# Sixty-four experts' weights in 2 MB transfers with 16 KB runs, VectorE's block transpose for the hidden layer, and a ring of ten matrices

## The chip, the cores and the metric

The kernel runs on one core of a Trainium2 chip. The metric is the device time of one execution in microseconds; the time before is the median of three runs. One execution was also recorded by the hardware profiler, and all rows below are from that record. In it PE is TensorE's matmul stream, PEld its weight loads, DVE is VectorE, ACT ScalarE, POOL GpSimd, and SP is SyncE, whose queue issues nearly all DMA transfers.

## The reference

One layer of a streaming encoder on 256 tokens of 1024 features, float32: a gated merge of two recurrent branches, a cross-attention over 256 memory tokens, and a mixture of 64 experts, of which each token takes two. The change lies in the last part:

```
def expert_block(args):
    xb, e = args
    hid = jax.nn.silu(xb @ w_gate[e]) * (xb @ w_up[e])      # [1024, 512] each
    return hid @ w_down[e]                                   # [512, 1024]
```

The router takes the best group of eight experts and in it the best two; their rows come back weighted, and a last RMS norm follows. Each of an expert's three matrices has 2 MB (2,097,152 bytes), so all experts have 402.65 MB, and every expert is computed whether tokens chose it or not.

## The kernel before

**Stages.** Projections, branches, merge, attention and router take the first part of the span. Their weights go through two buffers named `raw` (L162), are split in two by ACT, DVE and POOL (`whl`, L169 and L170), and are used by PE (L178 to L180). Then the experts run one after the other, 0 to 63, each on 32 slots for tokens. An `overflow` loop (L1190, L1191) ahead of them takes experts with more tokens than slots; here it makes no pass that counts.

**One expert** (`expert`, L1150). `gate_up` (L1094) multiplies the tokens with gate, then with up, eight tiles of the features each, with four ranges of 128 columns on four quarters of the array. `hidden` takes silu(gate) * up: ACT's tanh (L1102), two DVE instructions (L1103, L1104), a PE transpose into PSUM (L1106) and an ACT copy back (L1107). `down` (L1115) multiplies with the third matrix, `to_rows` (L1120) copies the result to rows. After every fourth expert, `combine` (L1126 to L1131) adds four experts' rows to the tokens' sums and `prepare` gathers the next four experts' tokens (`gather`, L1077 to L1088). The last expert's `down` goes by four ranges of columns (`LAST`), so that its end can start before its last bytes land (`last`, L1267 to L1285).

**The ring.** The weights come through a ring of 21 places of 1 MB, 8 KB of each partition: nine (`ra`) where the early stages' buffers were, twelve (`rb`) where the middle stages' buffers were. `order` lists the twelve in the order in which what was there before is done with: places 0 to 2 were single buffers, 3 and 4 `raw`, 5 to 8 `whl`, 9 to 11 those of the attention. `load_next` (L1061, L1063, L1067) fetches half a matrix: for gate and up, 8 KB of each partition that lie together in memory; for down, two pieces of 4 KB (hidden row j * 128 + p on partition p). 21 halves are issued ahead of the experts, six more after each expert, all from SP, in the order of use. A place's next transfer waits until PE has read what is in it, and a transfer also waits until the one eight places earlier in the queue has landed.

**What sets the order.** The instructions' order on each engine is chosen by a planner at build time, by its own costs; each engine then runs its queue in order and waits on semaphores. SP's queue therefore holds the ring's first transfers between the `raw` loads of the attention's weights, where the planner put them.

The lines that matter:

```
if i < 2:
    nc.sync.dma_start(t, src.rearrange("(p c) f -> p (c f)", p=128)[:, h * 2048:h * 2048 + 2048])
elif e < NE - 1:
    nc.sync.dma_start(t.rearrange("p (j n) -> p j n", j=2),
                      src[h * 256:h * 256 + 256].rearrange("(j p) n -> p j n", p=128))
```

Of the kernel before, what the change touches and what calls it, by code (L numbers as in the profile page):

```python
# [8 lines left out]
FT = mybir.dt.float32  # L9
# [13 lines left out]
# columns of the constants' arrays: for the whole, and for what comes before the attention  # L23
# [12 lines left out]
# columns of the small parameters' array  # L36
# [5 lines left out]
def hybrid_kernel(ctx: ExitStack, tc: tile.TileContext, A, out, dbg=None, until=99):  # L42
# [45 lines left out]
    def bcast(ap, n):  # L88
        """ap[p, w] as [p, n, w], each alike."""
        return ap.rearrange("p (o w) -> p o w", o=1).to_broadcast([ap.shape[0], n, ap.shape[1]])  # L90

    def spread(ap, n):
        """ap[p, w] as [p, w, n], each element n times."""
        return ap.rearrange("p (w o) -> p w o", o=1).to_broadcast([ap.shape[0], ap.shape[1], n])
# [32 lines left out]
    def rsqrt_columns(ys, xs, ts, y, x):  # L127
        """-8192 / sqrt(x) of x's columns xs, two instructions a step: the scale is squared away last."""
# [7 lines left out]
    def softplus(dst, x, t0, t1, t2):  # L136
        """max(x, 0) + log(1 + e), e = exp(-|x|), log(1 + e) = 2 atanh(e / (2 + e)) by its series."""
# [19 lines left out]
    def load_w(src, k=8, m=256, hi=(SC, SC), lo=(V, G), loads=1):  # L157
        """A unit of weights, [128, k, m], loaded and split: piece i // (k / 2) has its k-tile i."""
# [15 lines left out]
    def dense(p, w, m, u, k=8):  # L174
        """p[128 outputs of tile m, 256 tokens]; u(half, k-tile) is [128, 256]."""
# [6 lines left out]
    def dense_two(w, u):  # L182
        """Both tiles of a unit, a bank each, with what comes last of u used last."""
# [10 lines left out]
    def act(pair):  # L194
        """Halves in two tiles [128, 2048] as dense() takes them."""
        h = [t.rearrange("p (c t) -> p c t", c=8) for t in pair]
        return lambda s, i: h[s][:, i]
# [10 lines left out]
    def square_sums(xt, name):  # L208
        """[128 features of a tile, 256 tokens], summed over the tiles."""
# [7 lines left out]
    def rs_rows(x):  # L217
        """1 / RMS of each token, a row on every partition."""
# [52 lines left out]
    X = small("xg", [3, 2, 8])            # g cumulated in the chunk; g to its end; 2 beta  # L271
# [17 lines left out]
    EGL = small("egl", [2, 2, 8])         # exp of a chunk's whole decay: tile, half, head  # L289
    SC.activation(EGL.rearrange("p t c h -> p (t c h)"), pg[:, 32:64], AF.Exp)  # L290
    # A unit is a pair of heads and a chunk, a head on each half of the partitions:
    # [(head of the pair, token), quantity, (tile, pair, chunk of the tile)]
# [8 lines left out]
    TM = small("tm", [6, 16])             # g, g to the end, 2 beta, exp of the first two, -exp(g) / 4  # L301
# [52 lines left out]
    gg = [five("gg0"), five("gg1")]       # 2 gelu(rg)  # L354
# [15 lines left out]
    for h in range(2):  # L370
# [8 lines left out]
        # log a = ch (tr + 1), ch = -4 softplus(-lambda); -expm1(log a) = (1 + exp(log a)) tanh(-log a / 2)  # L379
# [5 lines left out]
        V.scalar_tensor_tensor(tr, a, 1.0, tr, op0=OP.add, op1=OP.mult)             # 1 - a  # L385
        V.tensor_scalar(a, tr, -1.0, 1.0, op0=OP.mult, op1=OP.add)
        V.scalar_tensor_tensor(tr, tr, -2.0, tr, op0=OP.add, op1=OP.mult)           # a^2 - 1
        # halved twice: for the gate's and for the gelu's halves
# [44 lines left out]
    gb = single("gb", 0).rearrange("p (c t) -> p c t", c=8)                         # tanh(gB / 2)  # L433
# [15 lines left out]
    # [side, pair of heads, chunk, head of the pair, 64 tokens]  # L449
# [43 lines left out]
    # a quarter, as k is doubled  # L493
    V.tensor_scalar(NK[:, 0], NK[:, 0], 0.25, EPS, op0=OP.mult, op1=OP.add)
    rsqrt(NK[:, 2], NK[:, 0], NK[:, 3])
    V.tensor_mul(NK[:, 3], NK[:, 2], NK[:, 2])                       # 1 / (sum k^2 + eps)
    V.scalar_tensor_tensor(NK[:, 5], TM[:, 2], 0.5, NK[:, 3], op0=OP.mult, op1=OP.mult)
    V.tensor_scalar_mul(NK[:, 6], NK[:, 5], 0.25)
    V.scalar_tensor_tensor(NK[:, 4], NK[:, 0], 0.5, NK[:, 2], op0=OP.mult, op1=OP.mult)   # its root, for v, which is doubled

# [27 lines left out]
    # a tile's diagonal blocks of 16 in columns (column of the block, its place in its 32, unit)  # L528
# [40 lines left out]
    # what the tensor engine does while it waits for the inverses  # L569
# [10 lines left out]
    flat8 = lambda t: t.rearrange("p n i -> p (n i)")  # L580

    def products(a, b):
        """a^T b of every unit, a's heads as diagonal blocks: a bank for eight units."""
# [8 lines left out]
    for lev in (16, 32):  # L592
# [5 lines left out]
        for g in range(2):  # L598
            if lev == 16:
                V.tensor_copy(US[:, GR[g]], p[g])  # L600
                # the blocks inverted so far lie within 32 x 32
# [27 lines left out]
    # o stands 4 sqrt(128 (sum q^2 + eps)) too large: its norm's eps is scaled alike  # L629
# [25 lines left out]
    for c in range(4):  # L655
# [47 lines left out]
        # the head's RMS norm  # L703
# [12 lines left out]
    def y_of_b():  # L716
        """Branch B's y, from o transposed."""
# [24 lines left out]
    for c0, n in ((0, 2), (2, 2), (4, 2), (6, 1), (7, 1)):  # L742
# [7 lines left out]
        with tc.high_priority():  # L750
            t = t2k("mrg")[:, :n * 256].rearrange("p (m t) -> p m t", m=n)
            V.scalar_tensor_tensor(t, gb[:, q], 1.0, pv, op0=OP.add, op1=OP.mult)
            V.tensor_add(t, t, ya[:, q])                             # doubled
# [43 lines left out]
    def scores(hq):  # L797
        """Two heads' scores and their softmax over the memory."""
# [19 lines left out]
    def turned(h):  # L818
        """A head's probabilities, transposed."""
# [15 lines left out]
    for un_ in range(4):  # L835
# [9 lines left out]
        if un_ == 0:  # L845
# [5 lines left out]
            V.tensor_scalar_mul(rs2[:, 1], rs2[:, 1], 1.0 / 16)      # with the scores' scale  # L851
# [196 lines left out]
    def load_next():  # L1048
        """Half of a matrix of an expert: four tiles of the features, two of the hidden ones."""
        n = len(ring)  # L1050
        if n >= 6 * NE:
            return
# [338 lines left out]
```

## Time and profile before

| what | value |
|---|---|
| time, median of 3 runs | 1516.94 us (1515.17 to 1519.67) |
| profiled execution: span from first to last instruction | 1514.2 us |
| profiled execution: own time | given as its span alone; the median lies 2.7 us above it |
| PE busy | 1188.8 us, 79% of the span |
| DVE, ACT, POOL busy | 519.3, 367.8 and 197.6 us |
| DMA queue of SP | 472.57 MB in 84048 packets, 78.6% of 16 engines' span |
| mean granted TensorE clock | 0.851 of full speed |

The page cuts the span into 40 slices of 37.9 us each; a digit is the busy share in tenths. A packet is what one DMA engine moves in one piece. The chain of waits starts at the last instruction and goes back, at each step, to what released it. In lists of instructions, "x32" is the number merged into the row, and what stands in brackets is the idle time before it and what ended it.

### The profile page before, as it was taken

What the parts mean: (1) busy time and instruction counts of PE and PEld (TensorE: products, weight loads), DVE (VectorE), ACT (ScalarE), POOL (GpSimd) and SP (SyncE); (2) the same over time, 40 slices, a digit from 0 to 9 for tenths busy, and PEclk for the clock granted to TensorE, in tenths of its full rate; (3) what the DMA queues carried; (4) which work ended last, traced back from release to release, by engine and by line L of the source; (5) the groups of instructions that cost most, each with busy time, mean ns of one, the idle gap of its engine ahead of it and who ended that gap; (6) DMA issues with size and microseconds to landing.
All of it is one profiled execution on the core that took longest, in us unless ns stands there. A gap on an engine that the chain in (4) does not pass through costs nothing.

```text
span 1514.2 us, 33706 instructions
## 1 busy us (share of the span) xinstructions
PE 1188.8 (79%) x15005; PEld 926.6 (61%) x15005; DVE 519.3 (34%) x1153; ACT 367.8 (24%) x810; POOL 197.6 (13%) x107
## 2 busy tenths in 40 slices
PE   6899889889998979877677686776777766768675
PEld 6898889789798966655344453444545434445343
DVE  7867788674666431211011110111101101111022
ACT  5366655425444421110000000100000000000002
POOL 2343333531136210000000000000000000000000
PEclk9899999979999989998787877777868778777787
DMA  7353344421157869999999999999999999999995
GB/s 255 124 176 127 124 145 145 157 84 56 56 196 277 342 224 372 415 415 416 415 415 416 417 415 415 415 416 415 416 415 416 416 417 413 417 411 414 415 409 208
DMA packets 85492, 477.44 MB, mean 315 GB/s; under 512 B 7520, under 2 KB 10208, under 8 KB 45152
## 3 DMA queue, kind: packets, MB, share of 16 engines
q1 hardware_dynamic: 84048, 472.57, 78.6%
q8 instruction: 119, 1.95, 0.5%
q10 hardware_dynamic: 1296, 2.68, 0.5%
q14 instruction: 29, 0.24, 0.0%
HBM read 474.17 MB, written 1.05 MB: 314 GB/s over the span
## 4 chain that ended last, share of the span: by engine, by line
DMA 51%; PE 10%; ACT 1%; issue 1%; DVE 0%; DVEq 0%; SPq 0%; ACTq 0%
DMA rb<-weu 12%; DMA rb<-weg 9%; DMA rb<-wed 9%; DMA ra<-weg 8%; DMA ra<-weu 7%; DMA ra<-wed 5%; PE gd L1094 4%; PE gd L1085 2%; PE gd L1115 2%; PE mm L1131 1%; PE mm L1162 0%; PE sm L1077 0%; PE sm L1126 0%; ACT hid L1102 0%; PE gd L1106 0%
## 5 line engine op out<-in xcount | busy, mean ns | idle before, releaser
L1094 PE MATMUL gd<-rb,xy 128*32 128x128 f32 x4608 | 181.6, 314 | 89.2 <-DMA rb<-weu 53.2
L1094 PEld LDWEIGHTS gd<-rb,xy 128*32 128x32 f32 x4608 | 144.4, 125 | 131.9 <-DMA rb<-weu 69.7
L170 POOL TENSOR_TENSOR whl<-raw,whl 128x1024 fp32r<-128x1024 f32 (+1 forms) x66 | 159.6, 2419 | 341.9 <-ACT whl L169 341.8
L1094 PE MATMUL gd<-ra,xy 128*32 128x128 f32 x3456 | 139.0, 317 | 67.2 <-DMA ra<-weu 40.3
L1094 PEld LDWEIGHTS gd<-ra,xy 128*32 128x32 f32 x3456 | 109.9, 127 | 100.1 <-DMA ra<-weu 51.9
L178 PE MATMUL mm<-u1h,whl 128*128 128x256 f32 x544 | 162.6, 299 | 9.8 <-DVE cvt L313 9.8
L1103 DVE SCALAR_TENSOR_TENSOR hid<-hid,gd 128x128 f32<-128x128 f32 x64 | 18.4, 287 | 426.1 <-ACT hid L1102 426.1
L180 PE MATMUL mm<-u1h,whl 128*128 128x256 f32 x544 | 160.7, 295 | 2.6 <-DVE whl L170 2.5
L179 PE MATMUL mm<-u1l,whl 128*128 128x256 f32 x544 | 159.9, 294 | 0.0
L169 ACT CAST whl<-raw 128x1024 fp32r<-128x1024 f32 (+1 forms) x132 | 131.3, 1008 | 110.6 <-PE mm L180 84.4
L1120 DVE COPY xy<-gd 32x256 f32<-32x256 f32 x126 | 52.7, 418 | 233.2 <-PE gd L1115 211.8
L1102 ACT ACTIVATE hid<-gd 128x128 f32<-128x128 f32 x64 | 17.8, 278 | 460.0 <-PE gd L1094 460.0
L1120 ACT COPY xy<-gd 32x256 f32<-32x256 f32 x126 | 45.9, 364 | 303.6 <-DVE xy L1120 303.6
L1115 PE MATMUL gd<-rb,hid 128*32 128x256 f32 x1152 | 104.5, 511 | 16.4 <-ACT hid L1107 9.6
L178 PEld LDWEIGHTS mm<-u1h,whl 128*128 128x128 f32 x544 | 109.4, 201 | 12.3 <-issue 6.3
L180 PEld LDWEIGHTS mm<-u1h,whl 128*128 128x128 f32 x544 | 109.1, 201 | 5.0 <-DVE whl L170 2.9
L179 PEld LDWEIGHTS mm<-u1l,whl 128*128 128x128 f32 x544 | 109.2, 201 | 0.8 <-issue 0.2
L976 POOL TENSOR_TENSOR gpw<-goh,ew 128x512 f32<-128x512 f32 x8 | 8.4, 1048 | 745.7 <-PE sm L1126 702.5
L170 DVE TENSOR_TENSOR whl<-raw,whl 128x1024 fp32r<-128x1024 f32 (+1 forms) x66 | 85.0, 1289 | 58.9 <-ACT whl L169 58.6
L1115 PE MATMUL gd<-ra,hid 128*32 128x256 f32 x864 | 74.4, 491 | 11.2 <-ACT hid L1107 7.6
L1085 PEld LDWEIGHTS gd<-goh,hm 128*128 128x128 f32 x512 | 67.2, 203 | 23.5 <-issue 22.5
L1088 DVE SCALAR_TENSOR_TENSOR xy<-gd,vecs,rr 128x128 f32<-128x128 f32 x128 | 39.0, 346 | 123.1 <-PE gd L1085 123.0
(421 smaller groups left out, 1826.8 us busy)
## 6 DMA issues: line engine op xcount, KB each, us to landing
rb<-weu SPq DMA_DIRECT2D x72, 1024.0 KB, 20.0
rb<-wed SPq DMA_DIRECT2D x72, 1024.0 KB, 20.1
rb<-weg SPq DMA_DIRECT2D x72, 1024.0 KB, 20.0
ra<-weg SPq DMA_DIRECT2D x56, 1024.0 KB, 20.0
ra<-weu SPq DMA_DIRECT2D x56, 1024.0 KB, 20.0
ra<-wed SPq DMA_DIRECT2D x54, 1024.0 KB, 20.1
raw<-win SPq DMA_DIRECT2D x34, 1024.0 KB, 4.9
raw<-wkv SPq DMA_DIRECT2D x7, 1024.0 KB, 4.9
```

The source lines that it names most:

```text
L169: (hi[j].copy if hi[j] is SC else hi[j].tensor_copy)(w[:, 0], r)
L170: lo[j].tensor_sub(w[:, 1], r, w[:, 0].bitcast(FT))
L178: T.matmul(p, w(0, i, ms), u(0, i), start=(i == 0), stop=False)
L179: T.matmul(p, w(0, i, ms), u(1, i), start=False, stop=False)
L180: T.matmul(p, w(1, i, ms), u(0, i), start=False, stop=(i == k - 1))
L1085: T.matmul(o, hm[:, tt, c * 128:c * 128 + 128], g[:, tt], start=(tt == 0), stop=(tt == 1))
L1088: V.scalar_tensor_tensor(xe[:, c], p[:, m * 256:m * 256 + n], P("w3", c), rr, op0=OP.mult, op1=OP.mult)
L1094: m = T.matmul(p[32 * j:32 * j + 32, o:o + 128], x[:, c], w(c)[:, j * 128:j * 128 + 128], start=(c == 0), stop=(c == 7), tile_position=(0, ...
L1102: SC.activation(tg, p[:, :128], AF.Tanh, scale=0.5)
L1103: V.scalar_tensor_tensor(th, tg, 1.0, p[:, :128], op0=OP.add, op1=OP.mult)
L1115: T.matmul(p[32 * q:32 * q + 32, :256], ht[:, 32 * j:32 * j + 32], w(j)[:, o:o + 256], start=(j == 0), stop=(j == 3), tile_position=(0, 32 ...
L1120: (SC.copy if q % 2 else V.tensor_copy)(Y[r:r + 32, q * 256:q * 256 + 256], p[32 * q:32 * q + 32, :256])
```

## The change

Each matrix is one transfer of 2 MB, in which each partition takes 16 KB that lie together in memory. Gate and up were laid out in that way before and came in two halves. For down the rows are now taken as hidden row p * 4 + j on partition p, so the hidden layer has to arrive in that order: the product of silu(gate) and up is written with the columns permuted (a, j to j, a), and VectorE's transpose of 32 x 32 blocks turns it, in place of PE's transpose and ACT's copy. The ring has ten places of 2 MB, four in `ra` and six in `rb`, each of the latter on two neighbours of the old twelve, and one of 1 MB (`half`) that is used once: it takes the first half of the eleventh matrix (expert 3's up), whose second half goes to the first place when that is free. The loop ahead of the experts calls `load_next` once more than there are places, and each expert calls it three times. The last expert's down comes in the same four ranges of columns. At the end, the tile for the final norm's weights (`nf`) takes the 1 MB place. Comments and docstrings were removed, which changes nothing.

```diff
-    NA, NB = 9, 12
+    NA, NB = 4, 6
...
+    rh = ctx.enter_context(tc.tile_pool(name="rh", bufs=1, side="right", reuse_waits="tile"))
...
-    free = [rb.tile([128, 2048], FT, name="rb", tag=f"rb{k}") for k in range(NB)]
-    order = (1, 0, 11, 10, 3, 4, 8, 5, 7, 6, 2, 9)
+    free = [rb.tile([128, 4096], FT, name="rb", tag=f"rb{k}") for k in range(NB)]
+    order = (0, 5, 2, 3, 1, 4)
+    half = rh.tile([128, 2048], FT, name="rh")
+    by_halves = A["weu"][(NA + NB) // 3].rearrange("(p c) f -> p (c f)", p=128)
...
+    def load_next():
+        n = len(ring)
+        if n >= 3 * NE:
+            return
+        e, i = divmod(n, 3)
+        src = A[("weg", "weu", "wed")[i]][e]
+        if n == NA + NB:
+            t = [half, place(n)]
+            nc.sync.dma_start(t[1][:, :2048], by_halves[:, 2048:])
+            ring.append(lambda c: t[c // 4][:, c % 4 * 512:c % 4 * 512 + 512])
+            return
+        t = place(n)
+        if i < 2:
+            nc.sync.dma_start(t, src.rearrange("(p c) f -> p (c f)", p=128))
+            ring.append(lambda c: t[:, c * 512:c * 512 + 512])
+        elif e < NE - 1:
+            nc.sync.dma_start(t, src.rearrange("(p j) n -> p (j n)", p=128))
+            ring.append(lambda j: t[:, j * 1024:j * 1024 + 1024])
+        else:
+            for q in LAST:
+                nc.sync.dma_start(last_columns(t, q), src[:, q].rearrange("(p j) n -> p j n", p=128))
+            ring.append(t)
...
-        V.tensor_mul(tg, th, p[:, 128:256])
-        pt = bank("gd")
-        T.transpose(pt[:, :128], tg, ident)
-        SC.copy(ht, pt[:, :128])
+        by4 = lambda a: a.rearrange("p (a j) -> p a j", j=4)
+        V.tensor_mul(tq.rearrange("p (j a) -> p a j", j=4), by4(th), by4(p[:, 128:256]))
+        V.transpose(ht, tq)
...
-    for _ in range(NA + NB):
+    for k in range(NA + NB + 1):
+        if k == NA:
+            nc.sync.dma_start(half, by_halves[:, :2048])
         load_next()
...
-            m = gate_up(p, k * 128, x, lambda c: w[2 * k + c // 4][:, c % 4], range(8))
+            m = gate_up(p, k * 128, x, ring[3 * e + k], range(8))
...
-        down(p, ht, lambda j: wd[j // 2][:, j % 2], range(4))
+        down(p, ht, ring[3 * e + 2], range(4))
...
-        for _ in range(6):
+        for _ in range(3):
             load_next()
...
-    nf, fo = [ra.tile([128, 2048], FT, name="ra") for _ in range(2)]      # those of an expert that is done
+    nf = rh.tile([128, 2048], FT, name="rh")
+    fo = ra.tile([128, 4096], FT, name="ra")[:, :2048]
```

## Rows read from the trace of the kernel before

**Rows 1.** The page's slices of the span: DMA share in tenths and rate.
```profile
DMA  7353344421157869999999999999999999999995
GB/s 255 124 176 127 124 145 145 157 84 56 56 196 277 342 224 372 415 415 416 415 415 416 417 415 415 415 416 415 416 415 416 416 417 413 417 411 414 415 409 208
```

**Rows 2.** The page's chain of waits, shares by engine.
```profile
DMA 51%; PE 10%; ACT 1%; issue 1%; DVE 0%; DVEq 0%; SPq 0%; ACTq 0%
```

**Rows 3.** Windows: length, busy us of PE, PEld, DVE, ACT, POOL; clock, DMA, GB/s.
```profile
658.00:960.00 302.00, 216.13 (x3430) 140.55 (x3422) 41.13 (x123) 27.60 (x90) 3.14 (x3) 0.79 1.02 416
```

**Rows 4.** Waits of SP's queue, 660 to 1480 us: total, times, longest.
```profile
SPq L1061 <- DMA rb<-weg: 134.8, 64, 2.9
```

**Rows 5.** SP's issues in order of time: start, us, transfer (two merged).
```profile
1008.88 2.88 SPq L1061 DMA_DIRECT2D rb<-weg  x2
1013.92 2.83 SPq L1061 DMA_DIRECT2D rb<-weu  x2
1018.90 2.87 SPq L1063 DMA_DIRECT2D rb<-wed  x2
1023.96 2.88 SPq L1061 DMA_DIRECT2D rb<-weg  x2
1028.99 2.82 SPq L1061 DMA_DIRECT2D rb<-weu  x2
```

**Rows 6.** DMA between 660 and 1480 us: packets by size, and code loading.
```profile
DMA packets 60355, 340.26 MB, mean 415 GB/s; under 512 B 5171, under 2 KB 5171, under 8 KB 32619
...
q8 instruction: 73, 1.20, 0.6%
```

**Rows 7.** SP's issues as the ring fills and as it starts again.
```profile
542.60 6.43 SPq L1063 DMA_DIRECT2D rb<-wed  x2
550.09 0.82 SPq L1061 DMA_DIRECT2D rb<-weg  x2
550.96 0.42 SPq L1061 DMA_DIRECT2D rb<-weu  x1
569.25 0.34 SPq L1061 DMA_DIRECT2D ra<-weu  x1
570.96 2.05 SPq L1063 DMA_DIRECT2D ra<-wed  x2
...
577.41 5.17 SPq L1061 DMA_DIRECT2D ra<-weu  x2
583.13 1.25 SPq L1063 DMA_DIRECT2D ra<-wed  x2
```

**Rows 8.** Windows while the ring fills and stands full (columns as rows 3).
```profile
550.00:562.00 12.00, 5.68 (x53) 4.26 (x51) 9.31 (x58) 1.31 (x7) 0.00 (x0) 0.72 0.87 345
562.00:571.00 9.00, 5.62 (x86) 3.90 (x82) 0.90 (x4) 0.47 (x1) 1.50 (x2) 0.50 0.13 25
```

**Rows 9.** The chain in order of time: expert 0's gate and up.
```profile
568.15 5.32 PE gd L1094 x108
```

**Rows 10.** What ACT's split of the weights waited for, 440 to 560 us.
```profile
  DMA raw<-wcq: 0.5, 1
```

**Rows 11.** PE's waits, 440 to 570 us, the longest.
```profile
PE sm L957 <- DVE ew L955: 6.3, 1, 6.3
```

**Rows 12.** Groups between 700 and 1400 us: count | busy us, mean ns.
```profile
L1106 PE MATMUL gd<-consts,hid 128*128 128x128 f32 x46 | 18.5, 402 | 36.1 <-DVE hid L1104 36.1
...
L1107 ACT COPY hid<-gd 128x128 f32<-128x128 f32 x46 | 12.2, 264 | 38.8 <-PE gd L1106 38.8
```

**Rows 13.** VectorE's block transpose in an early stage.
```profile
L550 DVE STREAM_TRANSPOSE sta<-sta 128x512 f32<-128x512 f32 x1 | 0.7, 698 | 0.0
```

**Rows 14.** PE at the end, in order of time.
```profile
1495.76 1.08 PE L1094 MATMUL gd<-ra,xy 128*32 128x128 f32 x32 [0.83 <-DMA ra<-weu]
...
1500.63 1.78 PE L1267 MATMUL gd<-ra,hid 128*32 128x384 f32 x16 [0.88 <-DMA ra<-wed]
```

**Rows 15.** PE in the stream, in order of time.
```profile
1006.30 1.93 PE L1094 MATMUL gd<-ra,xy 128*32 128x128 f32 x32 [1.73 <-DMA ra<-weu]
```

More of the change, by code (lines that the diff above doesn't have):

```diff
@@ L1046, in hybrid_kernel, with place @@
-    ring = []
+    free = [rb.tile([128, 4096], FT, name="rb", tag=f"rb{k}") for k in range(NB)]
+    order = (0, 5, 2, 3, 1, 4)
+    half = rh.tile([128, 2048], FT, name="rh")
+    by_halves = A["weu"][(NA + NB) // 3].rearrange("(p c) f -> p (c f)", p=128)
+    assert (NA + NB) % 3 == 1
+    ring = []
+    def place(n):
+        k = n % (NA + NB) - NA
+        if k < 0:
+            return ra.tile([128, 4096], FT, name="ra")
+        return free[order[k]] if n < NA + NB else rb.tile([128, 4096], FT, name="rb", tag=f"rb{order[k]}")
@@ L1048, in load_next @@
     def load_next():
         n = len(ring)
-        if n >= 6 * NE:
+        if n >= 3 * NE:
             return
-        e, i, h = n // 6, n // 2 % 3, n % 2
-        k = n % (NA + NB) - NA
-        if k < 0:
-            t = ra.tile([128, 2048], FT, name="ra")
-        else:
-            t = free[order[k]] if n < NA + NB else rb.tile([128, 2048], FT, name="rb", tag=f"rb{order[k]}")
-        src = A[("weg", "weu", "wed")[i]][e]
-        if i < 2:
-            nc.sync.dma_start(t, src.rearrange("(p c) f -> p (c f)", p=128)[:, h * 2048:h * 2048 + 2048])
-        elif e < NE - 1:
-            nc.sync.dma_start(t.rearrange("p (j n) -> p j n", j=2),
-                              src[h * 256:h * 256 + 256].rearrange("(j p) n -> p j n", p=128))
-        else:
-            for q in LAST[2 * h:2 * h + 2]:
-                nc.sync.dma_start(last_columns(t, q, h), src[:, q].rearrange("(j p) n -> p j n", p=128))
@@ L1068, in load_next @@
-        ring.append(t)
-    def last_columns(t, q, h):
-        return t[:, 4 * q.start - 2048 * h:4 * q.stop - 2048 * h].rearrange("p (j n) -> p j n", j=4)
+        e, i = divmod(n, 3)
[12 more added lines that the diff above has]
+            ring.append(lambda j: t[:, j * 1024:j * 1024 + 1024])
+        else:
+            for q in LAST:
+                nc.sync.dma_start(last_columns(t, q), src[:, q].rearrange("(p j) n -> p j n", p=128))
+            ring.append(t)
@@ L1073, in gather, with last_columns @@
+    def last_columns(t, q):
+        return t[:, 4 * q.start:4 * q.stop].rearrange("p (j n) -> p j n", j=4)
     def gather(xe, g, n):
@@ L1100, in hidden @@
         t = t2k("hid")
-        tg, th, ht = t[:, :128], t[:, 128:256], t[:, 256:384]
+        tg, th, tq, ht = [t[:, i * 128:i * 128 + 128] for i in range(4)]
         SC.activation(tg, p[:, :128], AF.Tanh, scale=0.5)
         V.scalar_tensor_tensor(th, tg, 1.0, p[:, :128], op0=OP.add, op1=OP.mult)
-        V.tensor_mul(tg, th, p[:, 128:256])
-        pt = bank("gd")
-        T.transpose(pt[:, :128], tg, ident)
-        SC.copy(ht, pt[:, :128])
+        by4 = lambda a: a.rearrange("p (a j) -> p a j", j=4)
+        V.tensor_mul(tq.rearrange("p (j a) -> p a j", j=4), by4(th), by4(p[:, 128:256]))
+        V.transpose(ht, tq)
         return ht
@@ L1152, in expert @@
         x = xe[:, :, i % 4 * 32:i % 4 * 32 + 32] if e else xe0
-        w = [t.rearrange("p (c f) -> p c f", c=4) for t in ring[6 * e:6 * e + 4]]
         p = bank("gd")
         for k in range(2):
-            m = gate_up(p, k * 128, x, lambda c: w[2 * k + c // 4][:, c % 4], range(8))
+            m = gate_up(p, k * 128, x, ring[3 * e + k], range(8))
         if e == 2:
@@ L1165, in expert @@
         if last:
-            return last(ht, [last_columns(ring[6 * e + 4 + q // 2], LAST[q], q // 2) for q in range(4)])
-        wd = [t.rearrange("p (j n) -> p j n", j=2) for t in ring[6 * e + 4:6 * e + 6]]
+            return last(ht, [last_columns(ring[3 * e + 2], q) for q in LAST])
         p = bank("gd")
-        down(p, ht, lambda j: wd[j // 2][:, j % 2], range(4))
+        down(p, ht, ring[3 * e + 2], range(4))
         to_rows(Y, 32 * (i % 4), p)
-        for _ in range(6):
+        for _ in range(3):
             load_next()
@@ L1220, in overflow @@
             p = bank("gd")
-            src = A["wed"][bass.ds(e, 1)].rearrange("o (j p) n -> p (o j) n", p=128)
+            src = A["wed"][bass.ds(e, 1)].rearrange("o (p j) n -> p (o j) n", p=128)
             for j in range(4):
```

## The prediction

> **What bounds the kernel now.** I read the slices of the page first: from the sixteenth slice on DMA stands at 9 and the rate at about 415 GB/s until the last slice, while PE has gaps [rows 1]. So the last 930 us of the 1514.2 us span are a stream. The shares of the chain of waits agree: DMA transfers of the experts' weights make 51% of it, PE 10% [rows 2]. The windows say how much cover there is: between 658 and 960 us the DMA share is 1.02, PE is busy 216.13 of 302 us (72%) at a granted clock of 0.79, DVE 14%, ACT 9% [rows 3]. Earlier PE still eats the 21 MB that were loaded ahead, but DMA stands at 9 there too, so that makes no difference to the end. What sets the end is: when the stream starts for good, how long the bytes take, and what follows the last byte.
>
> **Price of a transfer now.** SP issues a transfer when the one eight places earlier has landed: in the stream its longest waits, six groups, are for DMA, the first 64 times 2.1 us [rows 4]. Distances between its issues are therefore durations of landings [rows 5]. The distance from weu to wed covers two halves of gate or up: 1018.90 - 1013.92 = 4.98, so a = 2.49 us per MB. The distances from weg to weu and from wed to weg hold one half of each kind: 5.04 and 5.06, so b = 5.05 - 2.49 = 2.56 us per MB of wed; the next expert's distances (5.03) give 2.54, and I take 2.55. An expert is 4a + 2b = 15.06 us. The two kinds differ in the run that lies together: 8 KB of a partition against 4 KB, and the packets are cut alike: of 60355 packets 32619 are under 8 KB, 5171 of those under 512 B, which leaves about 27,450 of 4 KB and 27,740 of 8 KB [rows 6], half and half, as runs of those lengths would give. A MB is 8 packets of 8 KB or 16 of 4 KB on each of the 16 engines, so eight more packets cost 0.06 us: 7.5 ns each.
>
> **The stream after the change.** Every matrix is 128 runs of 16 KB: 4 packets per MB and engine if a run stays one packet. No row of this queue shows a packet of 16 KB, so I bound it. From the nearest row, four packets fewer than a: 2.49 - 0.03 = 2.46 us per MB, an expert 14.76 us. Best end: halving the count saves the full 0.06 again: 2.43, an expert 14.58. Worse end: no better than 8 KB, 2.49, an expert 14.94. I take 2.46. How many experts count: 21 of the 384 MB are loaded ahead before and after (9 + 12 places of 1 MB; 4 + 6 of 2 MB and the half), so 363 MB or 60.5 experts. 60.5 x 15.06 = 911 us of the 930 us; the other 19 us (code loading among it, 73 packets of 16.4 KB in 820 us [rows 6], start and end) I leave as they are. Saved: 60.5 x 0.30 = 18.2 us (best end 29, worse end 7.3). Half as many transfers also mean half as many completions and issues; SP waits 2.1 us of 2.5 anyway, and I count nothing.
>
> The Trainium skill, DMA: Bandwidth & Descriptors, section "Why small descriptors are slow", puts a fixed 3 cycles of 32 bytes on each packet. By it 4 KB against 8 KB would cost 1.2%, where the rows above show 2.4%; by the page 16 KB would give 2.476 us per MB, a saving of 12.5 us instead of 18.2. HBM Reference, section "Specifications (TRN2)", has a core alone at about 425 GB/s, bounded by its DMA engines; 1.0486 MB at that rate is 2.467 us, so the page would leave hardly any room beyond my figure, an estimate of 15.6 us saved. Both lie within the bounds above.
>
> **Start of the stream.** Before, the ring is full early: the last place is filled by an issue at 550.96 us [rows 7], and DMA runs at a share of only 0.13 between 562 and 571 us [rows 8]. After, places come free in pairs of the old ones, each with the later of its two: places 0, 5 and 2 when old 1 and 0, 11 and 10, 4 and 5 did (until 542.60), and 3, 1 and 4 only from 550.09 to 551 us [rows 7]. Three 2 MB transfers then start where 4 MB did: 6 x 2.49 = 15 us and about 2 us until the first lands, so about 567 us. That lies within the idle stretch; cover left, 4 us. Next the restart: the first half of expert 0's weg is read by PE at 569.25 and the second at 570.96, and each released a half's transfer [rows 7]. After, the whole matrix has to be read: 570.96, so 1.7 us later. Then the supply: 1 MB at 570.96, 2 MB when weu is read (573.5, end of 108 matmuls from 568.15 [rows 9]), 2 MB at 577.41, 2 MB at 583.13. At 2.5 us per MB the first 5 MB last until about 585.5, and the issue at 583.13 with 2 us of start just meets it. I count +1.7 us, and up to +4 if it does not.
>
> In the stages before, SP now puts 2 MB transfers between the raw loads of the attention's weights. ACT waited for such a load once in 440 to 560 us, for 0.5 us [rows 10], so the cover there is thin for one load and ample for the rest. PE's longest wait of that stretch, 6.3 us, is for the router's DVE work [rows 11], and none of its waits is for such weights. A MB more ahead of a load costs that load 2.5 us, of which I take nothing on the path (0 to +5).
>
> **In the stream PE and the hidden layer.** PE now waits for a whole matrix before its first matmul, and lags up to 2.5 us more. Behind it nothing waits but a place: two of the ten are spare to the eight transfers in flight, and with 40 us in flight a PE that is late by 20 us, more than an expert's whole work on it (72% of 15.06), starves nothing. Removed per expert: a PE transpose of 402 ns and an ACT copy of 264 ns [rows 12]. Added: VectorE's block transpose; the trace has it with 512 columns at 700 ns [rows 13], so 128 columns take between 0.18 and 0.7 us, and I take 0.25. The product now writes with a stride, for which I take nothing, and at most the 0.26 us that such a pass over 128 columns takes. All lies beside the stream, covered by the 28% that PE is idle; without that cover it would be a gain of 0.4 us per expert.
>
> **End.** Now: the last half of weu lands, PE does 32 matmul instructions in 1.08 us, the hidden layer follows, the first two column ranges are done, and PE waits until 1500.63 for the third [rows 14]. After, 64 instructions follow that landing, 1.08 us more (2.8 us more at the clock at which the same 32 took 1.93 us [rows 15]), less 0.45 us of the hidden layer. PE's wait of 0.88 us and what lies before it takes up the first; at the slower pace 1 to 2 us show. I take +1.0 (0 to +2).
>
> **Sum.** -18.2 + 1.7 + 1.0 = -15.5 us against the profiled execution: a span of 1514.2 becomes 1498.7. The median of the runs shown is 1516.9, 2.7 above the span; the same difference gives 1501.4.
>
> **Rivals.** *16 KB no cheaper than 8 KB*, because the run is cut into 8 KB packets and so the change does not do what it says for DMA, or because the engines are at their ceiling at 421 GB/s (a). For it: the rate is flat at 415 to 417 in nearly every slice [rows 1]. Against: 4 KB and 8 KB still differ. Saved 7.3, costs 2.7: -4.6, 1512.3 us. *Slower: a 16 KB packet costs more than its bytes.* It decides in the stream, from 15.06 / 24 = 0.628 us per packet and engine (two of 8 KB take 2.49 / 4 = 0.623), so 1% over two halves suffices. For it: the only 16.4 KB packets in the trace, code loading, take 0.6% of 16 engines over 820 us for 73, 1.08 us each [rows 6]; against: they go elsewhere. At 3% over two halves an expert takes 15.39 us: +20 and +2.7, 1539.6 us; at the full 1.08 us an expert would take 24 x 1.08 = 25.9 us, which I hold for excluded, since those packets share the engines with the stream while they are timed. *The ring fills late*: PE's attention stage waits for raw loads behind 2 MB ones and the last three places land after 571 us. For it: 4 us of cover; against: PE's waits there name none. Four such loads at 2.5 us, 10 us: 1511.4 us.
>
> **Chances.** Forecast 0.64, with 0.01 of it within 0.3%; no cheaper 0.19, half of it beyond 0.3% (4.6 us, about what a measurement of this kernel tells from no change); late ring 0.08, of which 0.06 faster and 0.02 the same; slower 0.09. Faster 0.63 + 0.095 + 0.06 = 0.785, same 0.01 + 0.095 + 0.02 = 0.125, slower 0.09. The range runs from the best end (-29 + 2.7, 1490.6), drawn in to 1492, to 1514, past the middles of the no-cheaper and the late-ring cases; some 2 in 10 lie outside.
>
> **What would show it.** Right: packets of 16 KB and half the count; the distance from weg to weu at 4.92 us and the same for all three matrices; a rate of about 424 GB/s in the slices from 600 us on; the first issue after the idle stretch near 571 us; the gap from the last landing to the end as now plus 1 us. Wrong: a packet count that shows 8 KB; a DMA share that falls below 1 after 600 us (then places, not bytes); PE waiting for raw loads before 550 us; or the distance unchanged at 4.98.

## The result, and the profile after

The changed kernel takes 1498.92 us (median of four runs, 1497.33 to 1500.7), the kernel before, measured beside it, 1518.02: a ratio of 0.987, 95% interval 0.9854 to 0.9886. In a second measurement, beside the experiments on the loop below, it was 1496.97 against 1519.1, 0.985 (0.983 to 0.9871). The profiled span went from 1514.2 to 1498.9 us, 15.3 us shorter. The forecast was a span of 1498.7 (15.5 shorter) and a time of 1501.4.

The two spans understate the gain. By the medians it is 19.1 us (the interval gives 17.3 to 22.2), and 22.1 in the second measurement. A time is 1.7 to 2.0 us more than its span in all executions on record but one, so the profiled one of before took about 1516 us, 2 less than its median, and that of after, 1500.7, was the slowest of its four. All times and ratios below are of fast runs; run 3 alone has slower ones, three of its six, and its profile is of one of them.

The page of the changed kernel: DMA share and rate of the slices, the packets, SP's queue, and the shares of the chain of waits.

```profile
DMA  6343444431147857999999999999999999999995
GB/s 253 118 170 132 138 144 134 148 113 57 38 162 300 327 212 304 426 424 426 426 425 426 425 427 425 425 427 426 425 426 425 427 425 425 426 426 427 426 425 195
DMA packets 42001, 477.40 MB, mean 318 GB/s; under 512 B 4480, under 2 KB 7168, under 8 KB 9856
...
q1 hardware_dynamic: 40560, 472.56, 77.0%
...
DMA 55%; PE 5%; issue 1%; SPq 1%; DVE 0%; ACT 0%; DVEq 0%; ACTq 0%
```

Against [rows 1, 2] the stream runs at 425 or 426 GB/s where it ran at 415 or 416, and the queue moves the same bytes in 40560 packets where it took 84048. DMA's part of the chain has grown, PE's has halved.

The stretch of [rows 3] and the two of [rows 8], in the same columns (length, busy us of PE, PEld, DVE, ACT and POOL, granted clock, DMA share, GB/s):

```profile
658.00:960.00 302.00, 197.79 (x3453) 146.15 (x3452) 50.69 (x148) 22.83 (x70) 3.15 (x3) 0.82 1.01 426
550.00:562.00 12.00, 5.67 (x50) 4.88 (x52) 8.04 (x51) 1.31 (x7) 0.00 (x0) 0.77 0.80 319
562.00:571.00 9.00, 2.57 (x29) 0.94 (x21) 2.19 (x10) 0.47 (x1) 1.50 (x2) 0.50 0.65 278
```

DMA is full in the stream and PE has more idle time than before. Between 562 and 571 us, where DMA stood nearly still before (0.13), the ring is now still being filled (0.65), and PE works for only 2.57 us instead of 5.62.

SP's issues in the stream, as in [rows 5]: start, us, transfer.

```profile
1002.47 0.33 SPq L1073 DMA_DIRECT2D ra<-weg  x1
1007.37 0.33 SPq L1073 DMA_DIRECT2D ra<-weu  x1
1012.30 0.33 SPq L1076 DMA_DIRECT2D rb<-wed  x1
1017.17 0.33 SPq L1073 DMA_DIRECT2D rb<-weg  x1
1022.09 0.33 SPq L1073 DMA_DIRECT2D rb<-weu  x1
```

A 2 MB matrix of any of the three kinds takes (1022.09 - 1002.47) / 4 = 4.905 us, 2.45 per MB. (Single distances are longer in both kernels: the next one here is 6.40 us, and before there is one of 5.78 at 1442.04; the end of this section counts them too.) DMA alone between 660 and 960 us, the queue's packets, MB and share of 16 engines:

```profile
DMA packets 8769, 127.72 MB, mean 426 GB/s; under 512 B 972, under 2 KB 972, under 8 KB 972
...
q1 hardware_dynamic: 8738, 127.24, 100.0%
```

Of the 8738 packets 972 are tiny; the other 7766 have 127.24 MB, 16.4 KB each: a run of 16 KB is one packet. 16 engines x 300 us / 7766 = 0.618 us each, where two packets of 8 KB take 2.49 / 4 = 0.623 and four of 4 KB 2.55 / 4 = 0.638.

SP's issues as the ring fills and restarts, as in [rows 7]; then what SP waited for there (total, times, longest); then PE from the router's last matmul to expert 0, as in [rows 9]:

```profile
551.37 0.33 SPq L1073 DMA_DIRECT2D rb<-weu  x1
551.75 0.42 SPq L1076 DMA_DIRECT2D rb<-wed  x1
552.22 0.42 SPq L1073 DMA_DIRECT2D rb<-weg  x1
576.46 0.34 SPq L1068 DMA_DIRECT2D ra<-weu  x1
578.51 0.33 SPq L1076 DMA_DIRECT2D ra<-wed  x1
582.16 0.33 SPq L1073 DMA_DIRECT2D ra<-weg  x1
```

```profile
SPq L1203 <- SPq L1203: 6.0, 2, 4.9
```

```profile
564.51 0.69 PE L1011 MATMUL gd<-consts,xs 128*128 128x128 f32 x2 [0.63 <-ACT xs L1008]
571.79 1.49 PE L1107 MATMUL gd<-ra,xe 128*32 128x128 f32 x21 [6.58 <-issue]
573.65 4.83 PE L1107 MATMUL gd<-ra,xe 128*32 128x128 f32 x107 [0.37 <-issue]
578.41 0.71 PE L1090 MATMUL sm<-goh,rs 128*128 128x128 f32 x4
```

The last three places are asked for when they were expected to come free, but the first refill goes out at 576.46 instead of 569.25. PE starts expert 0 at 571.79, 6.58 us after its last work on the router. Meanwhile SP stands at L1203, the entry of the overflow loop, for 6.0 us, 4.9 of them in one piece: two 2 MB landings lie that far apart. It goes on at 569.63, and the last landing is at 569.6 (the issue at 552.22 and 17.4 us).

The hidden layer's two new forms between 700 and 1400 us (against [rows 12, 13]) and PE at the end (against [rows 14]):

```profile
L1118 DVE TENSOR_TENSOR hid<-hid,gd 128x128 f32<-128x128 f32 x47 | 17.5, 372 | 1.6
L1119 DVE STREAM_TRANSPOSE hid<-hid 128x128 f32<-128x128 f32 x47 | 14.6, 311 | 1.6
```

```profile
1481.96 1.95 PE L1107 MATMUL gd<-ra,xy 128*32 128x128 f32 x64 [1.37 <-DMA ra<-weu]
1485.49 1.07 PE L1280 MATMUL gd<-ra,hid 128*32 128x256 f32 x16 [1.58 <-issue]
1486.83 1.14 PE L1280 MATMUL gd<-ra,hid 128*32 128x384 f32 x16 [0.27 <-DMA ra<-wed]
```

From the first refill to the third column range the change has made 1500.63 - 569.25 = 931.4 us into 1486.83 - 576.46 = 910.4, 21.0 less; from there to the end 13.6 into 12.1, 1.5 less; and the first refill is 7.2 later. That is the whole of the 15.3 us between these two executions.

### The profile page after: what moved, and what is told of

Read it like the earlier page. It is cut to its first block, busy times and chain, and to the rows that moved or that the text cites. A ratio compares the mean times of both kernels' runs of the same rounds, so it can differ in the third digit from the quotient of the medians.

```text
span 1498.9 us, 33205 instructions
## 1 busy us (share of the span) xinstructions
PE 1113.3 (74%) x14941; PEld 932.0 (62%) x14941; DVE 548.0 (37%) x1217; ACT 352.1 (23%) x746; POOL 197.5 (13%) x107
## 3 DMA queue, kind: packets, MB, share of 16 engines
q1 hardware_dynamic: 40560, 472.56, 77.0%
q8 instruction: 119, 1.95, 0.5%
HBM read 474.17 MB, written 1.05 MB: 317 GB/s over the span
## 4 chain that ended last, share of the span: by engine, by line
DMA 55%; PE 5%; issue 1%; SPq 1%; DVE 0%; ACT 0%; DVEq 0%; ACTq 0%
DMA rb<-weu 11%; DMA rb<-wed 11%; DMA rb<-weg 10%; DMA ra<-wed 10%; DMA ra<-weu 8%; DMA ra<-weg 5%; PE gd L1107 2%; PE gd L1127 1%; PE gd L1098 1%; SPq L1080 1%; PE mm L1175 0%; PE mm L1143 0%; ACT fsq L1296 0%; PE sm L1090 0%; PE gd L1280 0%
## 5 line engine op out<-in xcount | busy, mean ns | idle before, releaser
L1107 PEld LDWEIGHTS gd<-rb,xy 128*32 128x32 f32 x4864 | 162.2, 128 | 140.1 <-DMA rb<-weu 63.6
L1107 PE MATMUL gd<-ra,xy 128*32 128x128 f32 x3168 | 122.1, 320 | 76.7 <-DMA ra<-weu 39.3
L1107 PEld LDWEIGHTS gd<-ra,xy 128*32 128x32 f32 x3168 | 106.9, 129 | 94.5 <-DMA ra<-weu 44.9
L1127 PE MATMUL gd<-rb,hid 128*32 128x256 f32 x1216 | 89.8, 445 | 61.4 <-DMA rb<-wed 41.2
L1127 PEld LDWEIGHTS gd<-rb,hid 128*32 128x32 f32 x1216 | 45.8, 123 | 95.1 <-issue 62.3
L1127 PE MATMUL gd<-ra,hid 128*32 128x256 f32 x800 | 61.1, 456 | 36.5 <-DMA ra<-wed 23.7
L1098 PEld LDWEIGHTS gd<-goh,hm 128*128 128x128 f32 x512 | 61.0, 192 | 14.5 <-issue 14.5
```

The costliest lines, as they stand in the source:

```text
L1098: T.matmul(o, hm[:, tt, c * 128:c * 128 + 128], g[:, tt], start=(tt == 0), stop=(tt == 1))
L1107: m = T.matmul(p[32 * j:32 * j + 32, o:o + 128], x[:, c], w(c)[:, j * 128:j * 128 + 128], start=(c == 0), stop=(c == 7), tile_position=(0, ...
L1127: T.matmul(p[32 * q:32 * q + 32, :256], ht[:, 32 * j:32 * j + 32], w(j)[:, o:o + 256], start=(j == 0), stop=(j == 3), tile_position=(0, 32 ...
```

## The experiments

A number that repeats well is the span less the time of the first refill (SP's first issue into a place that PE has emptied), since 363 MB are then still to come: 945.0 us before and 922.4 after, 921.8 in the changed kernel's second profiled execution. The stages ahead scatter more: the router's last matmul (L1011) starts between 560.5 and 566.2 us.

| kernel | time, us | ratio to before (95%) | span | first refill | span less refill | packets of SP's queue |
|---|---|---|---|---|---|---|
| before | 1518.02 | 1 | 1514.2 | 569.25 | 945.0 | 84048 |
| changed | 1498.92 | 0.987 (0.9854 to 0.9886) | 1498.9 | 576.46 | 922.4 | 40560 |
| 1, pieces of 8 KB | 1513.09 | 0.9963 (0.9944 to 0.9982) | 1509.5 | 571.65 | 937.9 | 64880 |
| 2, pieces of 4 KB | 1538.49 | 1.0134 (1.0113 to 1.0154) | 1534.7 | 574.31 | 960.4 | 113520 |
| 3, 1 MB by halves of the partitions | 2207.03 | 1.4583 (1.4512 to 1.4653) | 2248.1 | 574.10 | 1674.0 | 43440 |
| 4, 1 MB by even and odd partitions | 1495.61 | 0.9865 (0.9841 to 0.9888) | 1493.8 | 572.04 | 921.8 | 43440 |
| 5, PE's transpose back | 1498.38 | 0.9875 (0.9858 to 0.9891) | 1502.4 | 578.59 | 923.8 | 40560 |
| 6, changed, no loop | 1490.22 | 0.9816 (0.9797 to 0.9835) | 1490.7 | 569.31 | 921.4 | 40560 |
| 7, before, no loop | 1513.65 | 0.9965 (0.9952 to 0.9978) | 1510.7 | 566.68 | 944.0 | 84048 |
| 8, one matrix behind the loop | 1498.57 | 0.9883 (0.9866 to 0.9901) | 1495.7 | 573.98 | 921.7 | 40560 |
| 9, two behind it | 1498.53 | 0.9879 (0.986 to 0.9897) | 1496.8 | 575.06 | 921.7 | 40560 |
| 10, one, 3 us later | 1498.84 | 0.9857 (0.9835 to 0.9879) | 1497.2 | 572.60 | 924.6 | 40560 |
| 11, one, 9 us later | 1504.47 | 0.9895 (0.9877 to 0.9913) | 1502.7 | 574.79 | 927.9 | 40560 |

**1 and 2: packets alone.** Theory: the stream's gain lies in the number of packets. Rival: in larger transfers. Places, transfers and their order stay; only the run that lies together is cut (2 pieces, then 4).

```diff
-            nc.sync.dma_start(t, src.rearrange("(p c) f -> p (c f)", p=128))
+            nc.sync.dma_start(t.rearrange("p (h x) -> p h x", h=2),
+                              src.rearrange("(h p c) f -> p h (c f)", h=2, p=128))
```

> Changed kernel, but each 2 MB transfer takes two pieces of 8 KB for every partition, 1 MB apart in memory, where it took one of 16 KB; places, transfers, their order and their count stay. The rows of a matrix come to other partitions, so the experts' products are not the reference's. Theory (the stream's gain is in the number of packets): the 16 KB packets become pairs of 8 KB ones, a MB costs what gate's and up's cost in the kernel before, 2.49 us instead of 2.448; an expert takes 14.94 us instead of 14.69, and 60.5 of them add 15 us: about 1514 us. Rival (the gain is in larger transfers: half as many issues and completions, 16 MB instead of 8 MB in flight): nothing changes, 1499 us within 2 us.

> Changed kernel, but each 2 MB transfer takes four pieces of 4 KB for every partition; the rest as in the run with pieces of 8 KB, and again the experts' products are not the reference's. Theory (number of packets): 2.55 us per MB as down cost in the kernel before, an expert 15.30 us, 60.5 x 0.61 = 37 us more: about 1536 us, slower than the kernel before by some 18 us. Rival (larger transfers): 1499 us within 2 us.

Measured 1513.09 and 1538.49 us, where the theory had 1514 and 1536. Behind the first refill the stretch grows from 922.4 to 937.9 and 960.4. 180 of the matrices that are cut come behind the first refill, each with 128 packets more, then 256 more again, 8 and 16 on an engine: 15.5 us / 1440 = 10.8 ns, then 22.5 us / 2880 = 7.8 ns for a packet. The kernel before with its mixed runs lies between (945.0). The rival is excluded.

No other part of the layout shows. Between 660 and 960 us the queue moved 127.24, 125.33 and 121.98 MB with runs of 16, 8 and 4 KB. Two thirds of the bytes at the second rate and one third at the third would make 124.2 MB, and the kernel before, which has just this mix but other places in memory and transfers of 1 MB, moved 124.20. As every run was one packet, these runs can't tell a price of the packet from a gain of the longer run in memory.

**3 and 4: size of a transfer.** The same 16 KB packets, in transfers of 1 MB.

```diff
+        parts = (slice(0, 64), slice(64, 128)) if n > NA + NB else (slice(0, 128),)
...
-            nc.sync.dma_start(t, src.rearrange("(p c) f -> p (c f)", p=128))
+            for o in parts:
+                nc.sync.dma_start(t[o], src.rearrange("(p c) f -> p (c f)", p=128)[o])
```

> Changed kernel, but every matrix after the first eleven comes in two transfers of 1 MB, of 64 partitions each, still in runs of 16 KB; the filling of the ring stays. Theory (number of packets): the packets are the same, so 1499 us within 2 us, though SP issues twice as often. Rival (larger transfers): half the bytes in flight and twice the completions bring back 2.49 us per MB, 15 us more, 1514 us. A third outcome, that 64 partitions use fewer of the 16 engines, would show as a DMA share far below 1.

Neither: 2207.03 us. DMA between 660 and 960 us of this run (an execution of 2249.91 us):

```profile
DMA packets 4920, 64.50 MB, mean 215 GB/s; under 512 B 983, under 2 KB 983, under 8 KB 983
...
q1 hardware_dynamic: 4905, 64.26, 100.6%
```

All 16 engines are busy, and each packet takes twice its time: 16 x 300 / (4905 - 983) = 1.22 us. So the third outcome was wrong too in its sign, a low DMA share. The next run takes the even partitions, then the odd ones: `(slice(0, 128, 2), slice(1, 128, 2))`.

> As the run with transfers of 1 MB, but one transfer takes the even partitions and the next the odd ones, so each is spread over all 128. In that run the packets of 16 KB took 1.2 us instead of 0.614 at a full DMA share; theory there: 64 neighbouring partitions take writes at half the rate. If so, here the packets are back at about 0.61 us, and with them the question that run left open is answered: if only packets count, 1499 us within 2 us; if the size of a transfer counts, up to 15 us more, 1514 us. Rival (any transfer of 64 partitions is slow, whichever they are): above 2200 us again.

```profile
DMA packets 9731, 127.59 MB, mean 425 GB/s; under 512 B 1942, under 2 KB 1942, under 8 KB 1942
...
q1 hardware_dynamic: 9699, 127.10, 100.0%
```

Full rate, and 921.8 us behind the first refill as in the changed kernel. Twice the issues and completions and half the bytes in flight cost nothing that these runs can tell (1495.61 us). The gain is in the packets.

**5: the hidden layer.** PE's transpose and ACT's copy back in place of VectorE's transpose.

```diff
-        V.tensor_mul(tq.rearrange("p (j a) -> p a j", j=4), by4(th), by4(p[:, 128:256]))
-        V.transpose(ht, tq)
+        V.tensor_mul(tq, th, p[:, 128:256])
+        pt = bank("gd")
+        T.transpose(pt[:, :128], tq, ident)
+        SC.copy(ht, pt[:, :128])
```

> Changed kernel with PE's transpose and ACT's copy back in the hidden layer and VectorE's block transpose gone; the hidden rows then stand in another order than the third matrix's, so the experts' products are not the reference's. Theory (the hidden layer lies beside the stream): no change in the stream, about 0.4 us more behind the last landing of up, of which the last matrix's own landing hides most: 1499 us within 1.5 us. Rival (the layer's shorter path or PE's free time matters): 0.4 us for each of 64 experts, 25 us more, 1524 us.

0.9875 against 0.987 and 0.985, 1498.38 us where the theory had 1499: no difference that these runs can tell. It lies beside the stream. (Its one profiled execution is 1.4 us longer behind the first refill than the changed kernel's.)

**6 and 7: the loop.** Theory: the first refill is late because the entry of the overflow loop waits for all ten landings. Both kernels were run without `overflow()`, run 6 the changed one, run 7 the one before.

> Changed kernel without the overflow loop, which makes no pass on this data; experts with more than 32 tokens would lose some. Theory (the entry to the loop waits until all ten matrices have landed, 569.6 us in the changed kernel's trace, and holds PE's first expert to 571.8 us): PE starts expert 0 when its tokens are there, near 565.7 us, the first transfer of the full ring is issued near 570.5 instead of 576.5, and the end comes 5 to 6 us earlier, about 1493 us. Rival (PE starts late because the attention stage and the router are late, by transfers of 2 MB ahead of theirs): the start moves by 1 us at most, 1498 us.

> Kernel before without the overflow loop, which makes no pass on this data; experts with more than 32 tokens would lose some. It shows how much of what the loop costs is new with the change. Theory (entry waits for the ring's landings, and these were over at 561.8 us when the loop was reached at 562.1 in the kernel before): only the loop's own instructions and the reload of PE's program go, from PE's start at 565.77 and its pause until 568.15 to a start near 564.5, so 2 to 4 us: about 1514 us, against 8.2 us in the changed kernel. Rival (the loop costs the same in both, so the late start of the changed kernel has another cause): 8 us less, 1510 us.

PE in the changed kernel without the loop, then in the kernel before without it:

```profile
564.45 0.63 PE L1011 MATMUL gd<-consts,xs 128*128 128x128 f32 x2
565.60 5.68 PE L1107 MATMUL gd<-ra,xe 128*32 128x128 f32 x128 [0.52 <-DVE xe L1012]
```

```profile
563.53 0.63 PE L1011 MATMUL gd<-consts,xs 128*128 128x128 f32 x2
564.68 5.76 PE L1094 MATMUL gd<-ra,xe 128*32 128x128 f32 x128 [0.52 <-DVE xe L1012]
```

PE starts when expert 0's tokens are there, so the attention stage and the router are not what is late. From L1011 to the first refill it is 4.86 us (569.31 - 564.45) and 3.15 us (566.68 - 563.53): the whole matrix instead of its half costs 1.7 us. With the loop it is 11.95 us in the changed kernel (10.27 in its second profiled execution) and 6.03 before. So the loop costs 7.1 (5.4) us there and 2.9 here; 2.5 to 4.2 us of it are new. Runs 1 to 5 have the same ten matrices ahead of the loop and take 10.2 to 12.4 us. In all these seven executions SP leaves the entry within 0.1 us of the last landing, and PE starts expert 0 1.05 us behind that landing in four of them and 2.1 to 2.6 us in three. So this wait holds PE, and in those three something more does (see runs 10 and 11). The times came out near the forecasts (1490.22 us for 1493, 1513.65 for 1514), but do not show the size of the new part: by the ratios the changed kernel gains 5 to 8 us without the loop, the kernel before 5.3 (3.3 to 7.3), a difference of 0 to 3 us.

**8 and 9: a matrix behind the loop.** If entry waits for landings, fewer transfers ahead of it should free PE.

```diff
-    for k in range(NA + NB + 1):
+    for k in range(NA + NB - 1):
...
     overflow()
+    for k in range(1 + 1):
+        load_next()
```

Run 9 has `NA + NB - 2` and `2 + 1` there.

> Changed kernel; the tenth matrix of the ring is asked for behind the overflow loop instead of ahead of it; nothing is left out. Theory (the loop is entered when the last matrix ahead of it has landed): it now waits for the ninth, which landed at 564.7 us instead of 569.6, so PE starts expert 0 some 4.5 us earlier (571.8 to about 567); DMA stands still for about 3 us around the loop and 1 us before the first refill instead of 9.5 us in one piece, 5 us less: about 1494 us. Rival (what the run without the loop saved was the loop's own instructions on the path, not its wait for landings): within 1 us of the changed kernel, 1498 to 1500 us.

> Changed kernel; the ninth and the tenth matrix are asked for behind the overflow loop. Theory (entry waits for landings): the eighth landed at 559.8, before the number of the loop's passes is known (562.8), so the entry waits for no landing and PE starts expert 0 near 565.8 us; but DMA stands still from 559.8 until the loop is left, about 566, and then the ring has 4 MB to take, which lasts past the first refill at 570.5: idle 6 us instead of 9.5, about 1495.5 us, worse than with one matrix behind the loop. Rival (loop's own instructions): 1498 us or, with DMA idle for longer, above 1500.

No gain: 0.9883 and 0.9879, 1498.57 and 1498.53 us, as the rival had it and not 1494 and 1495.5. SP at the loop in the run with one matrix behind it, its issues, and PE:

```profile
SPq L1203 <- SPq L1203: 0.8, 1, 0.8
```

```profile
562.65 0.34 SPq L1073 DMA_DIRECT2D rb<-weg  x1
573.98 0.33 SPq L1068 DMA_DIRECT2D ra<-weu  x1
```

```profile
560.47 0.69 PE L1011 MATMUL gd<-consts,xs 128*128 128x128 f32 x2 [0.64 <-ACT xs L1008]
566.02 1.50 PE L1107 MATMUL gd<-ra,xe 128*32 128x128 f32 x21 [4.87 <-issue]
571.18 4.85 PE L1107 MATMUL gd<-ra,xe 128*32 128x128 f32 x107 [3.66 <-issue]
```

The wait at the entry is gone (0.8 us instead of 6.0), as the theory had it. But PE starts 3.4 us after SP has left the loop and asked for the tenth matrix, and after 21 matmuls it stands for another 3.66 us, for nothing that these rows name. In the run with two behind the loop the two pauses are 4.48 and 3.91 us. The saved wait has turned into these. DMA in the second pause, 567.5 to 571.2 us (packets, MB, share of 16 engines), has one instruction load among the matrix's packets, which suggested the next theory, that PE fetches its program behind them:

```profile
q1 hardware_dynamic: 62, 0.75, 48.6%
q8 instruction: 1, 0.02, 1.6%
```

**10 and 11: the tenth matrix later still.** POOL writes part of its place first, so that SP has to wait (once; in run 11 three times).

```diff
+        if n == NA + NB - 1:
+            for k in range(1):
+                G.tensor_scalar_mul(t[:, k * 1024:k * 1024 + 1024], hm[:, 0], blk[:, 0:1])
```

> As the run with one matrix asked for behind the loop, but POOL first writes 1024 columns of that matrix's place (values of no use that the transfer overwrites), so that SP asks for it one to two us later. Theory (after the loop PE fetches its program by DMA, and in that run the fetch stood behind the tenth matrix's packets: PE started at 566.0, 3.9 us after SP left the loop, and after 21 matmuls paused 3.7 us more): the fetches get ahead of the matrix at least in part, PE reads expert 0's gate sooner, and a later transfer makes the kernel faster: 1496 to 1498 us where that run had 1498.6. Rival (PE's late start has nothing to do with the tenth matrix): 1 to 2 us slower, about 1500 us.

> The same with three such instructions, so that the tenth matrix is asked for four to six us after the loop, when PE has its program. Theory: PE's pause after 21 matmuls is down to about 0.4 to 0.9 us, as in the kernel before, its first matmul within 1 us of the loop's end; DMA stands still some 4 us longer ahead of the tenth matrix but no longer behind it: 1495 to 1497 us. Rival: 4 to 5 us slower than without the delay, about 1503 us.

> The changed kernel itself, on the chip and in the rounds of the three above, so that they are compared with it directly: 0.987 of the kernel before, 1498 to 1500 us, PE's first matmul of the experts behind the last landing of the ring.

POOL took 2.85 us for one and 8.49 for three, so the matrix was asked for at 570.08 and 574.41, some 3 and 9 us after the loop and not 1 to 2 and 4 to 6. PE in the first, then in the second:

```profile
565.15 0.69 PE L1011 MATMUL gd<-consts,xs 128*128 128x128 f32 x2 [0.63 <-ACT xs L1008]
567.70 1.50 PE L1110 MATMUL gd<-ra,xe 128*32 128x128 f32 x21 [1.86 <-DVEq L1206]
569.80 4.60 PE L1110 MATMUL gd<-ra,xe 128*32 128x128 f32 x107 [0.60 <-issue]
```

```profile
563.84 0.69 PE L1011 MATMUL gd<-consts,xs 128*128 128x128 f32 x2 [0.64 <-ACT xs L1008]
569.83 1.50 PE L1110 MATMUL gd<-ra,xe 128*32 128x128 f32 x21 [5.30 <-issue]
571.78 4.64 PE L1110 MATMUL gd<-ra,xe 128*32 128x128 f32 x107 [0.45 <-issue]
```

The times are 1498.84 us, between the theory's 1496 to 1498 and the rival's 1500, and 1504.47, where the theory had 1495 to 1497 and the rival 1503.

What the two pauses are can be read in the traces of all twelve executions with the loop. The page's queue q8 carries 119 loads of program (kind "instruction") of 16 KB each; PE with its weight loads has 29,882 of the 33,205 instructions, so I take q8 for PE's. PE has branches of its own at the loop's line; in the kernel before and in the changed one they took, in ns, shortest, median and longest:

```profile
L1191 PEldq COMPARE_BRANCH  x3: 97/187/413, 563.9 to 565.5; - x3
L1203 PEldq COMPARE_BRANCH  x3: 101/187/4987, 565.2 to 571.5; - x3
```

The longest one is the first pause. It takes 0.41 us in the kernel before and in run 10, where a load of 16 KB had ended 2.0 and 1.3 us before the branch began. In the ten other executions it takes 2.3 to 5.4 us (3.27, 2.89 and 3.78 in runs 8, 9 and 11) and ends 1.4 to 1.6 us behind the end of such a load, which began from 0.2 us before the branch to 2.8 us behind its start. The second pause, after 20 or 21 matmuls, ends 1.2 to 1.5 us behind the end of the next load in each of the eight executions that have one; in the other four (runs 1, 3 and 4 and the second execution of the changed kernel) that load was over before PE started.

The second pause follows the theory. With a matrix under way (runs 8 and 9) its load began 2.9 and 3.0 us behind PE's first matmul, and the pause is 3.66 and 3.91 us. In the six without one the load began from 0.5 us before that matmul to 0.04 us behind it, and the pause is 0.37 to 0.95 us: 0.37 in the changed kernel, 0.88 before (ahead of the row of [rows 9]). The first pause does not: in run 11 nothing was under way, the load began 0.9 us behind the branch, and PE still stood 3.78 us in it, 5.30 in all; in run 8 it began at 562.46, before the matrix was asked for. That half of the theory falls. The Trainium skill, Runtime: NRT & Kernel Launch, section "Instruction fetch mechanics", says that a taken branch out of the pages at hand makes the engine wait for a fetch; the traces agree with it, 2.3 to 5.4 us where the load came late and 0.41 us where it had come. Why it comes early in one execution and late in another stays open.

In the changed kernel the first pause is hidden in the wait for the landings, but for its end: PE's branch is over at 570.64, 1.0 us behind the last landing. So runs 8 and 9 took the wait away and got the pauses in its place. Runs 8 to 10 and the changed kernel have intervals that all overlap. Run 10 restarts 7.45 us after L1011, where the changed kernel took 10.27 and 11.95, and gives this back for the matrix that is missing from the ring (924.6 us behind the first refill). The changed kernel itself came out at 1496.97 there, 1 us under what was expected, its ratio of 0.985 with 0.987 inside the interval. No version that keeps the loop beats it clear of the noise.

## Why the prediction came out right

The time (1501.4 forecast, 1498.92 measured) and the cause were right. That the spans agree to 0.2 us (15.5 forecast, 15.3 measured) is luck: the start came 5.5 us later than forecast, the stream took 2.8 and the end 2.5 us less, and much of the start and nearly all of the end is how these two executions happened to run. By the medians the gain was 19.1 us, 3.6 more than forecast.

- **Price of a transfer.** Right in mechanism: all three matrices cost the same, the packets are 16 KB, and runs 1 to 4 show that the count of packets is what pays. The term was under-sized: 2.46 us per MB taken, 2.45 measured. Halving the count saved more than the 0.03 us that four packets at 7.5 ns would, because gate's and up's packets saved about 10 ns each (0.0375 us for four; 10.8 ns in run 1). An expert went from 15.06 to 6 x 2.4525 = 14.72 us, 0.345 and not 0.30; over 60.5 experts 20.9 us and not 18.2, and 21.0 is what the stretch lost. A hundredth of a microsecond per MB is 3.6 us here. The two savings worked out from pages of the Trainium skill (12.5 and 15.6 us) were both too small; the rate of about 425 GB/s for a core alone in the Trainium skill, HBM Reference, section "Specifications (TRN2)", agrees with the slices (424 to 427).
- **Start of the stream.** The step that failed. I had the last three landings at about 567 us (they were over at 569.6) and called the time until 571 cover, because PE would not read those matrices before. But something else waits for them, which the prediction did not count: the loop's entry, reached at about 563, which SP left at 569.63, so that PE started expert 0 at 571.79. The term of +1.7 us for the whole matrix is confirmed (4.86 against 3.15 us without the loop). To it come 4.2 us at the loop (2.5 in the second execution), and 1.3 us by which the router was later in this execution (564.51 against 563.22, within its scatter): 7.2.
- **Hidden layer and PE.** Right: run 5 shows no difference. VectorE's transpose took 0.311 us (0.25 taken), the strided product 0.372 instead of 0.287 (nothing taken), so an expert's hidden layer is 0.27 us shorter by these rows and not the 0.4 or 0.45 of the prediction. PE's idle share grew.
- **End.** +1.0 forecast, -1.5 measured. The 64 instructions took 1.95 us, as the prediction had it for the faster pace, and the wait for wed took them up (0.27 us of it is left). The rest is the granted clock in the execution of before. After PE had stood for 0.88 us it fell from 1.00 (2.4 GHz) to 0.50 (1.2 GHz), by the windows from 1501.0 to 1504.0 us: the third range took 1.78 us and the 16 matmuls behind it 3.17. After the change the clock stayed at 1.00 and they took 1.14 and 2.48: that is 1.3 us of the 1.5. It is no gain of the change: in the kernel before without the loop the same 16 matmuls took 2.49 us.
- **Rivals.** No cheaper than 8 KB: excluded, run 1 is the changed kernel with 8 KB packets and loses 14 us. A 16 KB packet that costs more: excluded, 0.618 us. The ring that fills late came true in part, but not through raw loads, of which PE waited for none; at 2.5 to 4.2 us it was smaller than its price of 10.

## What to carry to other kernels

Where DMA is full, read the price of a byte from distances between issues for each length of run, and lengthen the run before anything else: the size of a transfer did nothing here, the size of its packets 23 us (945.0 to 922.4 behind the first refill). Where transfers are moved later, ask not only who reads their data but which barrier waits for their landing; the entry of this loop waited for all. And where a wait is taken away, look at what stands behind it: here PE's program came as late as the landings, and nothing was gained. Hold each term of a sum against the trace, even where the sum fits, and against a second execution.

## What was not expected of the hardware

A transfer to 64 neighbouring partitions kept all 16 DMA engines busy and ran at half the rate (215 GB/s, 1.22 us for a packet of 16 KB); the same 64 packets to every other partition ran at 425 GB/s. The Trainium skill, SBUF — State Buffer, section "Door 1: The DMA port swizzle (why `[64,N]` ≈ `[32,N]`)", says that partitions 0 to 63 reach only half of the ports; both runs agree with it. And at a loop that makes no pass, PE stood 2.3 to 5.4 us in its own branch in ten of twelve executions, each time until 1.4 to 1.6 us behind the end of a 16 KB load of program, and up to 3.91 us more after 21 matmuls.
